# New costs in the account that sets the order of emission of a two-block transformer kernel

## The chip, the cores and the metric

The kernel runs on one NeuronCore of a Trainium2 chip. The metric is the device time of one execution in microseconds (us); several executions are timed and their median is given. TensorE appears in the rows as PE (matmuls) and PEld (weight loads), VectorE as DVE, ScalarE as ACT, GpSimd as POOL, SyncE as SP.

## The reference, cut to what matters

All arithmetic is float32, the batch is 1, the sequence 256 tokens, the model width 2048. A first block works on 272 positions (16 meta tokens ahead of the 256), then a second block of two layers on the 256.

```
block 1:  z  = rmsnorm(h) @ w_in                     # u 1024, q_a 512, kv_a 256, k_pe 64
          ya = s5_mixer(u)                           # 64 groups x 64 complex states
          yb = mla_mixer(q_a, kv_a, k_pe)            # 8 heads
          h += concat(rmsnorm(ya), rmsnorm(yb)) @ w_out
          h += conv_ffn(rmsnorm(h))                  # width 5504
s5_mixer: h[t] = lam_bar * h[t-1] + B u[t];  y = Re(C h) + d * u
          g = gelu(y);  out = g * sigmoid(g @ w_glu + b_glu)
block 2, twice: four mixers of four heads each on one projection (compressed, selected and
          windowed attention; stick breaking; forgetting; differential), w_out,
          then a gated feed-forward net of width 5632 with a convolution of 3 taps
```

The S5 mixer is a linear recurrence along the sequence. Its result passes a GELU before the product with `w_glu` can begin.

## The kernel before, in words

Activations lie transposed in SBUF: features on the 128 partitions, positions along the free axis. Each weight matrix streams in from HBM in halves of 128x1024 floats. A float32 product is made of three passes of the type float32r: the operand is split into a high part (ScalarE copies it to `wh`) and a remainder (VectorE, seldom GpSimd, subtracts: `wl`), and `mm3` issues high by high, low by high and high by low, the lines 633, 634 and 635 of the profile. One 128x512 piece of a weight, one `wh` and one `wl`, feeds 12 passes. `split` makes the pieces and `next` hands them out, up to six pieces ahead (`lead`) in eight buffers.

The instructions of each engine run in the order in which the program emits them (the schedule is manual), so the order of emission is the schedule. Python generators produce it. A main stream emits the big products; beside it stand "sides", generators that emit the S5 steps, the attention heads, the evacuations of PSUM and the norms. The main stream calls `pump` between its products, and `pump` advances every side that is ready.

What is ready is told by an account. Each engine has a clock: `t` for TensorE, `V.clk` for VectorE, `G.clk` for GpSimd, `H.clk` for ScalarE. Every instruction emitted moves the clock of its engine on by a cost worked out from its shape (`_Engine.cost` for the three vector-like engines; `mm`, `mm3`, `mm2` and `mm1` for TensorE), after the clocks at which its operands are written by the account (`_Model.run`). These clocks decide only three kinds of things. A side yields a delay, often `after(V)`: the time until `V.clk` plus 150 ns is reached by `t`. A side is held while `V.clk` or `H.clk` is more than 2700 ns ahead of `t` (`_ok`); the S5 steps have a stricter test, 2500 ns, called `calm`, and the GpSimd part of a step (`post`) is held while `G.clk` is over 1000 ns ahead. And `split` gives a `wl` to GpSimd if `G.clk` is at most 300 ns ahead of `t` and `V.clk` at least 800 ns (in block 1 alone). When the main stream needs a result of a side, `run_until` lets `t` run in steps of 100 ns until it has been emitted.

Block 1 up to the GLU is where most kinds of work run side by side. The main stream emits the projections: u (four pairs of output tiles), q_a, kv_a, k_pe, then the second projections of q, k and v. The S5 side makes 16 steps beside it, two for each tile of 128 channels. A step s is: `bu` (eight TensorE instructions into PSUM banks 4 and 5, operands `s5e` and `s5B`); on VectorE a multiply out of PSUM (`s5ab`), an add (`s5wr`), once more both, and four scans (`s5s`, 128x136); then on GpSimd, in `post`, a multiply `s5pb<-s5s,T` of 128x544 and an add of 128x272 written to a slot named `yl`, each twice. `bu` of step s+1 overwrites the PSUM that the second `s5ab` of step s reads; it is emitted `w_ = self.after(V, extra=0)` after that instruction. Beside the steps, `tables` makes the sines (`tba` and `T`, ScalarE and one VectorE operation per step) and `weights` makes the coefficients of each tile (`s5sm`, `s5C`, GpSimd). After every second step `out` multiplies by C on TensorE. The main stream then comes to the GLU: `gpre` waits until the GELUs of the eight tiles are emitted, so until the last S5 step has been. From there on come the GLU, the product with `w_out` with the attention beside it, and the feed-forward net.

In block 2 the four mixers are sides beside the projections. The stick-breaking mixer (`mix_b`) has a scan of 128x384 for each head, eight in all. GpSimd has little to do there.

Of the kernel before, what the change touches and what calls it, by code (L numbers as in the profile page):

```python
# [25 lines left out]
PSUM = bass.MemoryType.PSUM  # L26
# [262 lines left out]
class _Model:  # L289
# [18 lines left out]
    def run(self, clk, eng, outs, ins, cost, done=60.0):  # L308

        for ap in ins:  # L310
            for k in self.keys(ap):
                w = self.wr.get(k)
                if w is not None:
                    clk = max(clk, w[0] + (0.0 if w[1] == eng else 100.0))
        ok = [k for ap in outs for k in self.keys(ap)]
        for k in ok:
            for d in (self.rd, self.wr):
                w = d.get(k)
                if w is not None and w[1] != eng:
                    clk = max(clk, w[0] + 60.0)  # L320
        clk += cost
        for ap in ins:
            for k in self.keys(ap):
                self.rd[k] = (clk, eng)
        for k in ok:
            self.wr[k] = (clk + done, eng)
        return clk
# [16 lines left out]
class _Engine:  # L344
# [7 lines left out]
    def cost(self, name, out, ins, kw, a):  # L352
        n = 1
        for d in out.shape[1:]:
            n *= d
        if self.name == "V":
            fast = name in ("tensor_scalar", "tensor_copy", "memset") and not any(x.space == PSUM for x in ins)
            return 70.0 + n * (0.52 if fast else 1.04) + (60.0 if name == "tensor_tensor_reduce" else 0.0)
        if self.name == "G":
            if any(isinstance(x, OP) and x == OP.pow for x in a):  # L360
                return 300.0 + 165.0 * n
            return 130.0 + n * (2.15 if len(ins) > 1 else 1.1)
        c = 82.0 if ins and ins[0].space == PSUM else 125.0
        c += 93.0 * sum(not isinstance(kw.get(x, 0.0), (int, float)) for x in ("scale", "bias", "accum_out"))
        f = [x for x in a if isinstance(x, AF) and x in _SETS]
        if f and _SETS[f[0]] != self.set:
            self.set = _SETS[f[0]]
            c += 1283.0
        return c + 0.714 * n

    def __getattr__(self, name):
        f = getattr(self.eng, name)

        def call(out, *a, **kw):
            isap = lambda x: hasattr(x, "ap") and hasattr(x, "space")
            outs = [out] + ([kw["accum_out"]] if "accum_out" in kw else [])
            ins = [x for x in a if isap(x)] + [x for n, x in kw.items() if n != "accum_out" and isap(x)]
            if name == "tensor_tensor_reduce":
                outs.append(ins.pop())
            self.clk = self.k.model.run(self.clk, self.name, outs, ins, self.cost(name, out, ins, kw, a))  # L380
            return f(out, *a, **kw)  # L381

        return call
# [7 lines left out]
class Kern:  # L391
# [109 lines left out]
    def after(self, *engines, extra=150):  # L501

        return max([e.clk for e in engines]) + extra - self.t

    def mm(self, out, lhsT, rhs, start=True, stop=True, n=None, **kw):
        n = n or out.shape[-1]
        if lhsT.dtype != F32:
            c = max(107.0, n / 2.4 + 2.5)
        elif "tile_position" in kw:
            c = 40.0 + 0.4 * n  # L510
        else:
            c = 400.0 if n < 8 else max(220.0, 1.655 * n)
        self.t = self.model.run(self.t, "P", [out], [lhsT, rhs], c)
        self.nc.tensor.matmul(out, lhsT, rhs, start=start, stop=stop, skip_group_check=True, **kw)  # L514
# [114 lines left out]
    def mm3(self, acc, wh, wl, xh, xl, start, stop):  # L629
        nc = self.nc  # L630
        n = acc.shape[-1]
        self.t = self.model.run(self.t, "P", [acc], [wh, wl, xh, xl], 3 * max(109.0, n / 2.4 + 2.5))
        nc.tensor.matmul(acc, wh, xh, start=start, stop=False, skip_group_check=True)  # L633
        nc.tensor.matmul(acc, wl, xh, start=False, stop=False, skip_group_check=True)  # L634
        nc.tensor.matmul(acc, wh, xl, start=False, stop=stop, skip_group_check=True)  # L635

    def mm2(self, acc, wh, wl, xh, start):
        self.t = self.model.run(self.t, "P", [acc], [wh, wl, xh], 2 * max(109.0, acc.shape[-1] / 2.4 + 2.5))
        self.nc.tensor.matmul(acc, wh, xh, start=start, stop=False, skip_group_check=True)
        self.nc.tensor.matmul(acc, wl, xh, start=False, stop=False, skip_group_check=True)  # L640

    def mm1(self, acc, wh, xl):
        self.t = self.model.run(self.t, "P", [acc], [wh, xl], max(109.0, acc.shape[-1] / 2.4 + 2.5))
        self.nc.tensor.matmul(acc, wh, xl, start=False, stop=False, skip_group_check=True)

    def acc4(self, b, n):
# [1787 lines left out]
```

## Time and profile before

| | us |
|---|---|
| median of 3 executions | 3526.95 (3524.05 to 3529.26) |
| profiled execution, its own time | 3522.4 |
| span of the profile, first to last instruction | 3520.6 |
| mean granted TensorE clock, share of full speed | 0.983 |

The profile is one execution. Its own time is 1.8 us above its span. All figures of single instructions come from it, and sums over stages are sums within its span. An instruction that the helper of line 381 emits (all of VectorE, ScalarE and GpSimd) shows that one line, so groups are told apart by the names of their tiles.

### The profile page before, as it was taken

How to read it: one execution, taken by the hardware profiler on the slowest of the kernel's cores; microseconds unless marked ns; L12 is line 12 of the kernel's file. 1: busy time of each engine (PE TensorE's matmuls, PEld its weight loads, DVE VectorE, ACT ScalarE, POOL GpSimd, SP SyncE). 2: the span in 40 equal slices, each digit the busy share in tenths (PEclk: the TensorE clock that was granted, in tenths of full speed). 3: DMA queues.
4: the chain of work that ended last, by engine and by line, in shares of the span. 5: the costliest groups of instructions: out<-in, count | busy, mean ns of one | idle time of the engine just before them, and what ended most of it. 6: DMA issues, size and time to landing. Idle time of an engine off the chain costs nothing.

```text
span 3520.6 us, 70757 instructions
## 1 busy us (share of the span) xinstructions
PE 3391.7 (96%) x27971; PEld 3271.2 (93%) x27971; DVE 2427.7 (69%) x4598; ACT 1714.2 (49%) x3445; POOL 501.0 (14%) x547
## 2 busy tenths in 40 slices
PE   7879999999999999999999999989999999999997
PEld 6768999999999888898999999988899899999997
DVE  7996766666655756558887785565665788888655
ACT  5445544344455555465444444454455544444554
POOL 5652300000000200012000000030000300000002
PEclk9889999999999999999999999999999999999999
DMA  5323455555655564564665556646455455555663
GB/s 176 113 73 104 157 192 177 183 187 176 200 193 184 175 203 151 160 200 147 206 199 194 194 192 194 194 136 230 148 176 171 147 194 195 195 198 195 198 195 126
DMA packets 175022, 618.55 MB, mean 176 GB/s; under 512 B 20224, under 2 KB 24464, under 8 KB 174432
## 3 DMA queue, kind: packets, MB, share of 16 engines
q1 hardware_dynamic: 173488, 612.55, 53.3%
q8 instruction: 219, 3.59, 0.4%
q0 software_dynamic: 336, 0.77, 0.1%
q14 instruction: 115, 0.94, 0.1%
q10 hardware_dynamic: 864, 0.70, 0.1%
HBM read 610.72 MB, written 2.10 MB: 174 GB/s over the span
## 4 chain that ended last, share of the span: by engine, by line
PE 85%; DVE 3%; issue 1%; POOL 1%; ACT 1%; DMA 1%; SPq 0%; ACTq 0%; POOLq 0%; DVEq 0%
PE ps L633 27%; PE ps L634 27%; PE ps L635 27%; PE ps L514 4%; DVE wl L381 1%; POOL acc L381 1%; PE ps L519 1%; DVE X L381 1%; DVE xl L381 0%; DMA wr<-in_w_dram 0%; DVE hb L381 0%; ACT wh L381 0%; DVE xh L381 0%; POOL X L381 0%; ACT hb L381 0%
## 5 line engine op out<-in xcount | busy, mean ns | idle before, releaser
L381 DVE TENSOR_TENSOR wl<-wr,wh 128x512 fp32r<-128x512 f32 (+1 forms) x2000 | 1373.9, 715 | 752.1 <-ACT wh L381 749.1
L381 ACT ACTIVATE wh<-wr 128x512 fp32r<-128x512 f32 (+1 forms) x2014 | 1194.7, 623 | 811.4 <-PE ps L635 378.6
L633 PE MATMUL ps<-xh,wh 128*128 128x256 f32 (+2 forms) x4876 | 1380.2, 283 | 18.1 <-ACT xh L381 8.1
L635 PE MATMUL ps<-xl,wh 128*128 128x256 f32 (+2 forms) x4980 | 1394.0, 280 | 2.9 <-DVE xl L381 2.9
L634 PE MATMUL ps<-xh,wl 128*128 128x256 f32 (+2 forms) x4876 | 1368.2, 281 | 10.8 <-DVE wl L381 10.6
L633 PEld LDWEIGHTS ps<-xh,wh 128*128 128x128 f32 x4876 | 926.9, 190 | 33.1 <-issue 9.7
L635 PEld LDWEIGHTS ps<-xl,wh 128*128 128x128 f32 x4980 | 945.2, 190 | 4.0 <-DVE xl L381 3.8
L634 PEld LDWEIGHTS ps<-xh,wl 128*128 128x128 f32 x4876 | 926.1, 190 | 16.7 <-DVE wl L381 14.8
L633 PE MATMUL ps<-hhh,wh 128*128 128x256 f32 x1820 | 502.1, 276 | 2.3 <-ACT y L381 1.5
L635 PE MATMUL ps<-hhl,wh 128*128 128x256 f32 x1820 | 501.8, 276 | 0.2 <-DVE hhl L381 0.2
L634 PE MATMUL ps<-hhh,wl 128*128 128x256 f32 x1820 | 501.6, 276 | 0.0
L633 PEld LDWEIGHTS ps<-hhh,wh 128*128 128x128 f32 x1820 | 341.7, 188 | 2.7 <-ACT y L381 1.7
L635 PEld LDWEIGHTS ps<-hhl,wh 128*128 128x128 f32 x1820 | 341.6, 188 | 0.4 <-DVE hhl L381 0.4
L634 PEld LDWEIGHTS ps<-hhh,wl 128*128 128x128 f32 x1820 | 341.7, 188 | 0.0
L381 POOL TENSOR_TENSOR acc<-acc,sq 128x256 f32<-128x256 f32 (+1 forms) x137 | 119.2, 870 | 1120.4 <-ACT sq L381 1115.3
L633 PE MATMUL ps<-yh,wh 128*128 128x258 f32 (+2 forms) x696 | 202.3, 291 | 12.4 <-DVE xl L381 8.4
L381 POOL TENSOR_TENSOR hh<-cv,cv 128x256 f32<-128x256 f32 x88 | 84.9, 965 | 852.1 <-DVE cv L381 820.0
L635 PE MATMUL ps<-yl,wh 128*128 128x258 f32 (+2 forms) x696 | 197.9, 284 | 1.7 <-DVE yl L381 1.7
L634 PE MATMUL ps<-yh,wl 128*128 128x258 f32 (+2 forms) x696 | 197.5, 284 | 0.0
L381 DVE SCALAR_TENSOR_TENSOR cv<-pad,cw,cv 128x256 f32<-128x256 f32 x352 | 180.8, 514 | 13.1
L635 PE MATMUL ps<-xl,wxh 128*128 128x256 f32 x588 | 163.9, 279 | 2.3 <-DVE xl L381 2.3
L381 DVE TENSOR_TENSOR wxl<-wr,wxh 128x512 fp32r<-128x512 f32 x230 | 162.6, 710 | 1.9 <-ACT wxh L381 1.9
(449 smaller groups left out, 4351.0 us busy)
## 6 DMA issues: line engine op xcount, KB each, us to landing
wr<-in_w_dram SPq DMA_DIRECT2D x1105, 512.0 KB, 4.7
wr<-in_cmpw_dram SPq DMA_DIRECT2D x32, 512.0 KB, 5.2
wr<-in_w_dram SPq DMA_DIRECT2D x16, 272.0 KB, 4.3
c2t<-in_c_dram SPq DMA_DIRECT2D x2, 1472.0 KB, 9.8
bc<-in_bc_dram SPq DMA_DIRECT2D x8, 256.0 KB, 3.6
X<-in_hT_dram SPq DMA_DIRECT2D x3, 544.0 KB, 9.8
out_dram<-X SPq DMA_DIRECT2D x5, 256.0 KB, 2.2
s5e<-yh SPq DMA_DIRECT2D x64, 17.0 KB, 2.2
```

The costliest lines, as they stand in the source:

```text
L381: return f(out, *a, **kw)
L514: self.nc.tensor.matmul(out, lhsT, rhs, start=start, stop=stop, skip_group_check=True, **kw)
L519: self.nc.tensor.transpose(out, in_, self.ident[:k, :k])
L633: nc.tensor.matmul(acc, wh, xh, start=start, stop=False, skip_group_check=True)
L634: nc.tensor.matmul(acc, wl, xh, start=False, stop=False, skip_group_check=True)
L635: nc.tensor.matmul(acc, wh, xl, start=False, stop=stop, skip_group_check=True)
```

## The change

Only the costs in the account change; no instruction is added, removed or given another shape. A scan is charged 130 + 2.08 n ns in place of 70 + 1.04 n. A VectorE operation with two or more SBUF tensor inputs and a cost over 150 ns is charged up to twice its cost while GpSimd's clock is ahead of VectorE's (`port`). A float32r pass of n columns is charged 113.5 ns per 256 columns, or 0.4427 n + 6, in place of n/2.4 + 2.5 (at least 107 or 109).

```diff
@@ _Engine.cost
         if self.name == "V":
+            if name == "tensor_tensor_scan":
+                return 130.0 + 2.08 * n
             fast = name in ("tensor_scalar", "tensor_copy", "memset") and not any(x.space == PSUM for x in ins)
             return 70.0 + n * (0.52 if fast else 1.04) + (60.0 if name == "tensor_tensor_reduce" else 0.0)
@@ _Engine
+    def port(self, ins, c):
+
+        g = self.k.G.clk - self.clk
+        if self.name == "V" and g > 0 and c > 150 and sum(x.space != PSUM and x.shape[-1] > 1 for x in ins) > 1:
+            return c + min(c, g)
+        return c
+
@@ _Engine.__getattr__, call
-            self.clk = self.k.model.run(self.clk, self.name, outs, ins, self.cost(name, out, ins, kw, a))
+            self.clk = self.k.model.run(self.clk, self.name, outs, ins, self.port(ins, self.cost(name, out, ins, kw, a)))
@@ Kern
+    def one(self, n):
+
+        return 113.5 * max(1.0, n / 256.0) if n % 256 == 0 else 0.4427 * n + 6.0
+
@@ mm
-            c = max(107.0, n / 2.4 + 2.5)
+            c = self.one(n)
@@ mm3 (mm2 and mm1 alike, with 2 and 1 passes)
-        self.t = self.model.run(self.t, "P", [acc], [wh, wl, xh, xl], 3 * max(109.0, n / 2.4 + 2.5))
+        self.t = self.model.run(self.t, "P", [acc], [wh, wl, xh, xl], 3 * self.one(n))
```

## Rows read from the trace of the kernel before

**Rows 1.** The page: busy time of the engines, then tenths busy in 40 slices.

```profile
PE 3391.7 (96%) x27971; PEld 3271.2 (93%) x27971; DVE 2427.7 (69%) x4598; ACT 1714.2 (49%) x3445; POOL 501.0 (14%) x547
...
PE   7879999999999999999999999989999999999997
...
DVE  7996766666655756558887785565665788888655
```

**Rows 2.** Windows: length, busy us (count) by engine, granted PE clock, DMA.

```profile
60.00:262.00 202.00, 158.07 (x1271) 140.60 (x1270) 184.84 (x309) 88.94 (x214) 135.01 (x135) 0.85 0.32 105
262.00:370.00 108.00, 106.78 (x719) 89.75 (x719) 70.67 (x218) 56.74 (x138) 30.09 (x32) 0.99 0.33 106
1200.00:1520.00 320.00, 313.50 (x2250) 277.18 (x2249) 193.02 (x459) 155.18 (x347) 12.53 (x11) 0.99 0.55 177
1640.00:2320.00 680.00, 678.33 (x5982) 677.93 (x5981) 494.32 (x893) 325.02 (x605) 48.62 (x50) 1.00 0.61 196
```

**Rows 3.** Waits from 60 to 262 us: total us, times, longest us.

```profile
ACT T L381 <- DVE tba L381: 51.8, 10, 9.1
POOL s5pb L381 <- DVE s5s L381: 26.6, 10, 5.1
...
PE ps L514 <- DVE s5ab L381: 24.5, 7, 5.7
...
DVE wl L381 <- ACT wh L381: 6.7, 4, 2.5
...
DVE yl L381 <- ACT yh L381: 3.4, 2, 2.2
```

**Rows 4.** DVE groups from 60 to 258 us: busy us, mean ns of one.

```profile
L381 DVE TENSOR_TENSOR wl<-wr,wh 128x512 fp32r<-128x512 f32 x58 | 57.7, 1006 | 6.8 <-ACT wh L381 6.7
L381 DVE TENSOR_TENSOR s5wr<-s5ab 128x272 f32<-128x272 f32 x32 | 33.4, 1042 | 1.1
L381 DVE TENSOR_TENSOR_SCAN s5s<-s5prm,s5wr 128x136 f32<-128x136 f32 x64 | 30.4, 534 | 0.1
L381 DVE TENSOR_TENSOR s5ab<-ps,T 128x544 f32<-128x544 f32 x32 | 23.0, 718 | 0.7
```

**Rows 5.** Tile s5s: ns min/median/max, first and last start.

```profile
L381 DVE TENSOR_TENSOR_SCAN s5s<-s5prm,s5wr x64: 407/416/1005, 69.4 to 254.7; 128x136 f32<-128x136 f32 x64
L381 POOL TENSOR_TENSOR s5pb<-s5s,T x32: 1329/1368/1691, 71.9 to 257.6; 128x544 f32<-128x544 f32 x32
```

**Rows 6.** Tile s5wr, 60 to 258 us, the adds.

```profile
L381 DVE TENSOR_TENSOR s5wr<-s5ab x32: 441/850/1577, 66.2 to 251.0; 128x272 f32<-128x272 f32 x32
```

**Rows 7.** Tile wl, 60 to 258 us, the VectorE subtractions.

```profile
L381 DVE TENSOR_TENSOR wl<-wr,wh x58: 659/795/1905, 59.4 to 257.7; 128x512 fp32r<-128x512 f32 x58
```

**Rows 8.** POOL groups from 60 to 258 us: busy us, mean ns of one.

```profile
L381 POOL TENSOR_TENSOR s5pb<-s5s,T 128x544 f32<-128x544 f32 x32 | 46.7, 1458 | 32.7 <-DVE s5s L381 26.6 <-PE ps L635 3.5 <-DVE tba L381 1.1
L381 POOL TENSOR_TENSOR yl<-s5pb 128x272 f32<-128x272 f32 x31 | 27.3, 882 | 2.4
...
L381 POOL TENSOR_TENSOR wl<-wr,wh 128x512 fp32r<-128x512 f32 x4 | 6.0, 1510 | 11.0 <-ACT wh L381 11.0
```

**Rows 9.** PE timeline, end of the S5 steps: start, us, instruction, idle before.

```profile
244.64 0.61 PE L514 MATMUL ps<-s5e,s5B 64*128 64x136 f32 x3 [0.86 <-DVE s5ab L381]
...
251.30 0.39 PE L635 MATMUL ps<-wl,yh 128*16 128x512 f32 x1
...
260.20 1.58 PE L514 MATMUL ps<-yl,s5C 128*32 128x135 f32 x22 [0.31 <-POOL yl L381]
261.71 0.58 PE L633 MATMUL ps<-yh,wh 128*128 128x258 f32 x1
```

**Rows 10.** DVE groups from 1200 to 1520 us, the scans of mix_b.

```profile
L381 DVE TENSOR_TENSOR_SCAN hb<-hb,c2t 128x384 f32<-128x384 f32 x4 | 3.8, 952 | 3.5 <-ACT hb L381 3.5
```

**Rows 11.** PE timeline, passes of 258 columns on end.

```profile
95.10 0.28 PE L635 MATMUL ps<-xl,wh 128*128 128x258 f32 x1
...
95.47 0.28 PE L635 MATMUL ps<-xl,wh 128*128 128x258 f32 x1
```

More of the change, by code (lines that the diff above doesn't have):

```diff
@@ L637, in mm2 @@
     def mm2(self, acc, wh, wl, xh, start):
-        self.t = self.model.run(self.t, "P", [acc], [wh, wl, xh], 2 * max(109.0, acc.shape[-1] / 2.4 + 2.5))
+        self.t = self.model.run(self.t, "P", [acc], [wh, wl, xh], 2 * self.one(acc.shape[-1]))
         self.nc.tensor.matmul(acc, wh, xh, start=start, stop=False, skip_group_check=True)
@@ L642, in mm1 @@
     def mm1(self, acc, wh, xl):
-        self.t = self.model.run(self.t, "P", [acc], [wh, xl], max(109.0, acc.shape[-1] / 2.4 + 2.5))
+        self.t = self.model.run(self.t, "P", [acc], [wh, xl], self.one(acc.shape[-1]))
         self.nc.tensor.matmul(acc, wh, xl, start=False, stop=False, skip_group_check=True)
```

## Prediction

> **What bounds the kernel now.** I read the page first: TensorE is busy 96% of the span, and its slices are full (8 or 9) everywhere but at the start and at a few short dips [rows 1]. The windows then say which stages have anything to give [rows 2]. From 1640 to 2320 us, a feed-forward stage, TensorE is busy 678.33 of 680 us; a new order can't shorten that. From 1200 to 1520 us, the mixers of the first layer (the second layer repeats it), TensorE idles 320 - 313.5 = 6.5 us. From 262 to 370 us it idles 1.2 us. The exception is 60 to 262 us, the S5 steps beside the projections: TensorE idles 202 - 158.07 = 43.9 us there, its granted clock is 0.85 on average, while VectorE is busy 184.84 of 202 us (92%) and GpSimd 135.01.
>
> So I asked for the waits of that stretch [rows 3]. TensorE's largest is 24.5 us in 7 waits at line 514, for `s5ab` on VectorE: `bu` of the next S5 step is emitted too early and the queue of TensorE stands. That looks like the prize, but its releaser is VectorE, which has hardly any idle time: 202 - 184.84 = 17.2 us, of which 6.7 and 3.4 us are waits for a copy of ScalarE (`wl` for `wh`, `yl` for `yh`). The stretch is bound by VectorE, and TensorE's idle time is what that leaves over. The timeline shows how the stretch ends [rows 9]: the last `bu` at 244.64 us, the last projection pass at 251.30, the last `out` at 260.20 behind GpSimd's add, and from 261.71 on the GLU. Main stream and S5 side end within 10 us of each other, and everything later follows the S5 side's end. What counts is when VectorE has done both lots of work.
>
> Much of VectorE's time is waiting inside instructions. A `wl` takes at least 659 ns and 1006 on average; an `s5wr` add 441 and 1042; a scan 407 and 534 [rows 4 to 7]. All three read two SBUF tensors, while `s5ab`, which reads one of its two from PSUM, shows nothing of the kind (718 ns). The excess over the minimum is 58 x 0.347 + 32 x 0.601 + 64 x 0.127 = 20.1 + 19.2 + 8.1 = 47 us of the 184.84.
>
> **The change part by part.** No instruction is added or removed, so every part acts through the order alone, and costs nothing where the order is not what ends the stage.
>
> *Scans.* The old charge for 136 columns is 70 + 1.04 x 136 = 211 ns, the new 130 + 2.08 x 136 = 413; the shortest in the trace is 407 and the median 416 [rows 5]. For 384 columns 469 becomes 929, and the trace has 952 [rows 10]. A step's four scans move `V.clk` on by 0.81 us more, 12.9 us over 16 steps.
>
> *Port.* Old charges: `wl` 602 ns, `s5wr` 353, scan 413 (new). With GpSimd's clock ahead each is up to doubled, which is about what the trace has (1006, 1042, 534). The account charges only when `G.clk` leads; as VectorE's clock grows faster now, GpSimd leads less often. Doubled for all of them it would be 58 x 0.602 + 32 x 0.353 + 64 x 0.413 = 73 us more, at the least 0; I take 15 us, a fifth, an estimate nearer the low end.
>
> *Passes.* The feed-forward stage has 680 us / 5982 = 113.7 ns for a pass, nearly all of 256 columns [rows 2]; the account goes from 109.2 to 113.5. For 258 columns it goes from 110 to 120.2; three passes on end take 0.37 us, 123 each [rows 11]. So `t` runs 4 to 9% faster against the other clocks, over some 100 us of block 1's projections about 9 us.
>
> What follows from 60 to 262 us, term by term:
>
> (a) `bu` is emitted later, after more passes, and the 24.5 us of waits shrink. Alone this is worth 0 at the end: VectorE is full while TensorE stands. Were VectorE not the bound, it would be up to 24.5; I take 0.
>
> (b) `tables` emits its sines behind `after(V)`. With a short `V.clk` they come too early into ScalarE's queue, which stands 51.8 us in 10 waits for `tba`; the copies `wh` queued behind reach VectorE late, the 6.7 and 3.4 us above [rows 3]. With a longer `V.clk` the sines come later. Between 0 and -10 us; I take -5.
>
> (c) A longer `V.clk` holds the S5 steps back by `calm` while the main stream is not held, so the main stream ends earlier against the S5 side, and the last few steps run with GpSimd as their bound. Per step GpSimd has 135.01 / 16 = 8.4 us; VectorE's own is (57.7 of `wl` left out) (33.4 + 30.4 + 23.0) / 16 = 5.4, with the small operations some 6.7 (estimate). Each step left over idles VectorE by about 8.4 - 6.7 = 1.7 us. Of extra work for VectorE in the account, 12.9 + 15 us, less the 9 us by which `t` is longer, 19 us remain; against 202 us over 16 steps, 12.6 each, that is one or two steps left over. Between 0 and 16 steps x 1.7 = 27 us; I take 2 steps, +3.
>
> (d) `split` gives a `wl` to GpSimd when VectorE's clock leads by 800 ns and GpSimd's by less than 300. VectorE leads more often, so I expect some three more than the 4 now [rows 8]. Each takes 1.0 us off VectorE and puts 1.5 on GpSimd, a third to two thirds of which comes back as waiting on the port. Between 0 and -6 us; I take -1.5.
>
> (e) Elsewhere: `t` 4% faster emits the attention's TensorE work a little early, which can add to the 6.5 us of idle in each layer; 0 to +3 for each, I take +0.5 for both together. The feed-forward stages are full and give 0; the cover there is TensorE's own queue.
>
> The sum is 0 - 5 + 3 - 1.5 + 0.5 = -3 us. Against the profiled execution's own 3522.4 us (span 3520.6 and 1.8 around it) that gives 3519.4. The median of the runs shown, 3526.95, lies 4.55 above that execution, so I predict 3524.
>
> **The rivals.**
>
> *Faster by more.* The accurate order keeps ScalarE and VectorE from standing at all (17.2 us of idle) and lets fewer two-input operations meet GpSimd. All of the idle and a tenth of the 47 us would be 22 us; two thirds of that, about -14, gives 3513. For it: the releasers of the idle are instructions emitted early. Against it: GpSimd has 135 us of work in 202 whatever the order, so most meetings stay.
>
> *Slower.* `calm` closes too long, and the S5 side falls far behind. In the tail a step alone is then a chain: 0.61 us of `bu` [rows 9], 2 x 0.72 + 2 x 0.44 of VectorE, 4 x 0.41 of scans, and on GpSimd (46.7 + 27.3) / 16 = 4.6, in all 9.2 us where VectorE has 6.7 to do, so 2.5 us lost a step. With 9 steps left over that is 22.5 us; less the 6.5 of (b) and (d), +16: 3543. It decides from about 6 steps left over, where 6 x 2.5 passes the 6.5 us gained and the 7 us of the bound below. Against it: evacuations and norms stop the main stream too by the same held sides, so the two can't part far.
>
> *GpSimd is held too.* The new account lets VectorE wait for GpSimd and not the reverse. The trace has `s5pb` at 1329 ns at least and 1458 on average [rows 5, 8], so GpSimd loses 32 x 0.13 = 4 us to something over the stretch, uncharged. If the held-back S5 steps gather at the end, where GpSimd is the bound, these 4 us come on top of (c): 3528. The Trainium skill has the rule ("SBUF — State Buffer", section "Who interferes with whom"): a VectorE instruction with two SBUF inputs and a GpSimd instruction that reads SBUF exclude each other, and the one that comes second waits until the first has ended. By that rule the trace agrees on both sides, 1006 ns against 659 for `wl` and 1458 against 1329 for `s5pb`, and an account with one side of it is half right.
>
> *Nothing moves.* The queues are ordered as before where it matters, and the time is 3527. The gates of the account work on differences of clocks, and all of them grow together.
>
> **How the numbers follow.** Forecast (-10 to +6 around -3) 0.40; faster by more 0.25; slower 0.20; GpSimd held too 0.08; nothing moves 0.07. A difference of 0.2%, 7 us, is about what a measurement can tell here. Of the forecast's own range some 0.11 lies beyond -7 and nothing beyond +6; the rest of it, GpSimd held too and nothing moves are within, 0.44, less 0.03 that GpSimd's 4 us may carry over the bound. Faster 0.36, same 0.41, slower 0.23. The range reaches halfway into both rivals and beyond: 3509 to 3541.
>
> **What the next profile would show.** Right: the 24.5 us of TensorE's waits for `s5ab` mostly gone; ScalarE's 51.8 us for `tba` lower; VectorE still about 90% busy between 60 us and the GLU, and the GLU's steady start within 7 us of 261.71; the last projection pass further ahead of the last `out` than 9 us; from there to the end the same length. Wrong: a start of the GLU 15 us away on either side, VectorE under 85% busy before it (the tail), or idle time of TensorE in the layers' mixers well over 6.5 us each.

## The result, and the profile after

The changed kernel takes 3549.01 us (median of 8 runs, 3541.05 to 3571.92); the kernel before, run beside it on the same chip, 3527.2 (8 runs, 3524.05 to 3529.97). The ratio is 1.0065, 95% interval 1.0046 to 1.0084: slower by 0.65%. The prediction was 3524 us, with a range of 3509 to 3541.

The profiled execution of the changed kernel is one of its longer ones: its own time is 3563.27 us, its span 3561.5. To see where it falls behind I used that each trace holds the same 26,148 passes of the main stream, so that the same pass can be looked up in any timeline. "The loss at pass N" below (counted from 1) is the start of pass N less its start in the kernel before. Two other kernels that keep the order of before in block 1 stand between -1.0 and +1.7 us up to pass 2401, so a loss of one or two microseconds can't be told from nothing.

| main stream's pass | where | before, us | loss after, us |
|---|---|---|---|
| 948 | last projection | 251.3 | 3.0 |
| 997 | GLU, running steadily in every trace | 268.1 | 11.0 |
| 1189 | `w_out`, behind its wait for the GLU's last results | 293.4 | 15.8 |
| 2401 | feed-forward of block 1 | 482.6 | 17.9 |
| 10,201 | end of the mixers, first layer | 1525.5 | 18.7 |
| 15,001 | up-projections of the first feed-forward net | 2086.8 | 38.9 |
| 26,148 | the last | 3500.7 | 40.9 |

So there are two losses: 17.9 us in block 1 up to the attention, and 20 us between 1525 and 2090 us, most of it at a steady rate. The second comes and goes between executions of one kernel (last section), so part of the 21.8 us between the medians is not the change's. Without it the shortest executions fit: 3541.05 - 3524.05 = 17.0 us. What has to be explained is block 1.

The windows of the changed kernel, same stretches as [rows 2] (length, busy us and count by engine, granted clock, DMA):

```profile
60.00:262.00 202.00, 159.98 (x1266) 143.19 (x1268) 182.79 (x295) 89.07 (x214) 134.04 (x135) 0.86 0.32 104
262.00:370.00 108.00, 97.92 (x653) 80.91 (x646) 69.72 (x197) 49.98 (x125) 33.20 (x31) 0.93 0.28 89
1200.00:1520.00 320.00, 313.99 (x2246) 277.05 (x2245) 197.32 (x469) 157.16 (x353) 13.97 (x14) 0.99 0.54 180
1640.00:2320.00 680.00, 676.98 (x5795) 676.28 (x5794) 491.52 (x888) 316.33 (x581) 48.45 (x54) 1.00 0.59 190
```

From 60 to 262 us nothing looks different by the shares: VectorE is 90% busy here as it was 92% before. But 295 of its instructions were run where 309 had been, in nearly the same busy time. From 262 to 370 us TensorE now idles 10.1 us where it idled 1.2, and its granted clock is 0.93 where it was 0.99: the S5 steps reach into that stretch.

The waits from 60 to 262 us, against [rows 3]:

```profile
ACT T L390 <- DVE tba L390: 45.9, 10, 8.9
...
POOL s5pb L390 <- DVE s5s L390: 15.7, 11, 4.9
DVE wl L390 <- ACT wh L390: 15.5, 9, 4.0
PE ps L527 <- DVE s5ab L390: 13.9, 4, 5.3
...
DVE yl L390 <- ACT yh L390: 1.0, 2, 0.8
```

The waits that the change was to remove did shrink: TensorE's for `s5ab` from 24.5 to 13.9 us, ScalarE's for `tba` from 51.8 to 45.9. VectorE's own wait for `wh` grew instead, from 6.7 to 15.5; that for `yh` went from 3.4 to 1.0.

The end of the S5 steps, against [rows 9] (timeline of TensorE):

```profile
254.27 0.39 PE L648 MATMUL ps<-wl,yh 128*16 128x512 f32 x1
256.37 1.19 PE L527 MATMUL ps<-s5e,s5B 64*128 64x136 f32 x8 [1.71 <-DVE s5ab L390]
...
274.77 1.13 PE L527 MATMUL ps<-yl,s5C 128*32 128x135 f32 x32
```

The last projection pass is 3.0 us later than before and the last `bu` 11.7; the last `out` ends at 275.90 us, 14.1 later.

VectorE is the busiest engine of the stretch, so its time up to the GLU is added up first. In the texts below "the GLU's start" is counted back from pass 997 by 48 passes of 0.12 us: 262.3 us before, 273.2 after. The windows from 0 to there, before and after:

```profile
0.00:262.30 262.30, 200.93 (x1561) 179.59 (x1562) 227.44 (x410) 125.09 (x295) 164.36 (x170) 0.89 0.37 121
```

```profile
0.00:273.20 273.20, 210.47 (x1551) 188.99 (x1552) 233.43 (x407) 125.16 (x295) 173.68 (x177) 0.86 0.35 116
```

Of the 10.9 us, VectorE's busy time makes 6.0 (227.4 to 233.4) and its idle time 4.9 (34.9 to 39.8). The two add up to the window by definition, so they divide the delay and do not explain it. The groups of VectorE in these windows show which instructions grew (busy us, mean ns; the scans and adds of before are those of [rows 4], its `wl` first here):

```profile
L381 DVE TENSOR_TENSOR wl<-wr,wh 128x512 fp32r<-128x512 f32 x81 | 75.1, 941 | 14.9 <-ACT wh L381 14.7
```

```profile
L390 DVE TENSOR_TENSOR wl<-wr,wh 128x512 fp32r<-128x512 f32 x76 | 69.1, 924 | 21.1 <-ACT wh L390 20.5 <-PE ps L648 0.4
L390 DVE TENSOR_TENSOR_SCAN s5s<-s5prm,s5wr 128x136 f32<-128x136 f32 x64 | 44.2, 748 | 0.0
L390 DVE TENSOR_TENSOR s5wr<-s5ab 128x272 f32<-128x272 f32 x32 | 31.2, 974 | 1.1
```

The same 64 scans take 44.2 us where they took 30.4. The tile's own view says how: the shortest is unchanged (407 ns in [rows 5]), the median nearly doubled from 416.

```profile
L390 DVE TENSOR_TENSOR_SCAN s5s<-s5prm,s5wr x64: 406/782/2048, 73.2 to 266.7; 128x136 f32<-128x136 f32 x64
```

Laid beside GpSimd's instructions, each of the 33 scans above 500 ns overlaps one of GpSimd, and of the 31 shorter ones 29 overlap none. Before there were 18 such long scans, again each with an overlap, and 44 of the other 46 had none. Overlaps with a `wl` on GpSimd went from 0 to 7, those with the S5 steps' own multiplies and adds (`s5pb<-s5s,T` and `yl`) from 3 to 14. The scans, the same 64 as before, gained 13.8 us of waiting, and `s5wr` lost 2.2. Of the 6.0 us that `wl` lost, 4.7 are its five instructions fewer (81 to 76, at 941 ns), and only 1.3 come from a shorter mean. The order that charges for meetings on the port has more of them, and the scans bear the increase.

### The profile page after: what moved, and what is told of

It reads as the page before. It is cut to its first block, busy times and chain, and to the rows that moved or that the text cites. A ratio compares the mean times of both kernels' runs of the same rounds, so it can differ in the third digit from the quotient of the medians.

```text
span 3561.5 us, 70788 instructions
## 1 busy us (share of the span) xinstructions
PE 3428.6 (96%) x27971; PEld 3305.4 (93%) x27971; DVE 2435.2 (68%) x4590; ACT 1714.9 (48%) x3445; POOL 510.8 (14%) x555
## 4 chain that ended last, share of the span: by engine, by line
PE 87%; DVE 7%; ACT 2%; issue 2%; POOL 2%; DMA 1%; SPq 0%; ACTq 0%; DVEq 0%; POOLq 0%
PE ps L646 27%; PE ps L648 27%; PE ps L647 27%; PE ps L527 5%; DVE wl L390 2%; DVE s5s L390 1%; POOL acc L390 1%; PE ps L532 1%; DVE X L390 1%; DVE xl L390 1%; ACT wh L390 1%; DVE s5ab L390 0%; DMA wr<-in_w_dram 0%; DVE s5wr L390 0%; DMA wr<-in_cmpw_dram 0%
## 5 line engine op out<-in xcount | busy, mean ns | idle before, releaser
L390 DVE TENSOR_TENSOR wl<-wr,wh 128x512 fp32r<-128x512 f32 x1992 | 1368.8, 716 | 780.4 <-ACT wh L390 776.6
L390 DVE SCALAR_TENSOR_TENSOR cv<-pad,cw,cv 128x256 f32<-128x256 f32 x352 | 180.8, 514 | 13.1
```

## The experiments

All kernels were timed beside the kernel before on one chip for each group: it took 3528.43 us with the first four, 3529.87 with the next four, then 3528.2, 3530.46 and 3528.96. The place of a loss was read from the passes of one profiled execution. The letters of the theories hold within one group. "The account" is the program that sets the order.

**Where: block 1 or the layers.** The new costs are applied only up to the end of the GLU's passes, or only from there on (A: the loss lies in block 1):

```
+    new = True                      # the other kernel: False
-            if name == "tensor_tensor_scan":
+            if self.k.new and name == "tensor_tensor_scan":
...
         s5st.close()                # end of the GLU's passes
+        self.new = False            # the other kernel: True
```

(`port` and `one` are switched in the same way.)

> New costs up to the end of the GLU, old costs from there on. Computes the same result. Theory A (the loss lies in the S5 stretch: the S5 steps are held back and end later, 277.6 us in the changed kernel's profile against 261.7): about 16 us slower than before, 3541 to 3546, and the steady start of the GLU near 277 us. Theory B (the loss is made in the layers, by attention work emitted early and by a slower rhythm of the passes there, 117.7 ns a pass against 113.3 in layer 0's feed-forward net): within 5 us of before, 3522 to 3532. If the executions spread as widely as the changed kernel's (3541 to 3572), the rhythm does not hang on the order in the layers.

> Old costs up to the end of the GLU, new costs from there on. Computes the same result. Theory A: the GLU's steady start stays at 262 us and the time at 3527, give or take 4. Theory B: 10 to 30 us slower, and as wide a spread as the changed kernel's 31 us.

The first took 3541.85 us (ratio 1.0031, 1.0007 to 1.0056) and has a loss of 10.6 us at pass 997 and 15.9 at pass 2401, nearly that of the changed kernel. The second took 3528.82 (0.9998, 0.9971 to 1.0025) and stays within 1 us of before at both passes. A was right on the time and the place (it had the GLU's start at 277 us, and it came at 272.9). The loss is made in block 1; in the layers the new costs do nothing that these times, good to some 0.25%, can tell.

**Which part.** Scans, port and passes one at a time, the other two with the old costs:

> Only the scans' new charge; port and passes as before. Computes the same result. Theory A1 (the longer scans hold the S5 side back most): last two S5 products on TensorE both after the last projection pass, GLU start at 270 us or later, 3535 to 3545. Theory A2 (the port charge does it): 3525 to 3531.

> Only the port charge; scans and passes as before. Computes the same result. Theory A1: 3525 to 3531. Theory A2: GLU start at 270 us or later, 3535 to 3545. If both this and the scans alone are slower, the two work through the same test of VectorE's clock and either is enough.

> The account of before, with the costs of the TensorE passes alone taken as new; all values are computed as before. By the account the sixteen bu are emitted after 258 to 888 passes of the main stream (before 264 to 930, after 252 to 948), and GpSimd is given 15 wl in block 1 (before 14, after 22). Theory A (what costs is that the account holds the S5 steps, so that the last one is emitted when the main stream has run out): last bu near 240 us as before, GLU start within 3 us of 261.7, time within 5 us of before. Theory B (what costs is the wl that GpSimd is given: each stretches scans on VectorE, which is the engine with the most work there): one wl more, so nothing either, within 5 us. Theory C (the true pass costs alone make the order worse): GLU start at 270 or later, 10 us or more above before.

Loss at passes 997 and 2401: scans 1.8 and 4.2 us (3527.0, ratio 0.9988, 0.9968 to 1.0009), port 3.2 and 6.0 (3529.84, 1.0005, 0.998 to 1.0029), passes 7.0 and 10.2 (3537.07, 1.0017, 0.9996 to 1.0039). Neither the scans nor the port alone makes the loss, so A1 and A2 are both out. The passes alone make half of it by another way: there the S5 steps are early (last `out` done at 259.2 us, before 261.8) and the projections late, pass 948 by 11.8 us. So the lateness of the S5 side, theory A of that group, isn't a necessary part; C was nearer, with 269.2 us where it asked for 270.

**GpSimd's subtractions, and the hold.** In the second group A says that steps held too long cost the time, B that the `wl` given to GpSimd stretch VectorE's scans. One number is changed in each:

```
 # kernel before
-        eng = ... self.V.clk >= self.t + 800 ...
+        eng = ... self.V.clk >= self.t + 300 ...
 # changed kernel
-        calm = lambda: V.clk <= self.t + 2500 and H.clk <= self.t + 2500
+        calm = lambda: V.clk <= self.t + 3500 and H.clk <= self.t + 3500
 # changed kernel
-        eng = ... self.V.clk >= self.t + 800 ...
+        eng = ... self.V.clk >= self.t + 1500 ...
```

> The kernel before with one number changed: split gives a wl to GpSimd when VectorE's clock is 300 ns ahead, where it was 800 ns. By the account the sixteen bu keep their places (264 to 930 passes) and GpSimd gets 20 wl instead of 14. Theory A (held steps): same places, so no loss, within 3 us of before, GLU start at 261 to 263 us. Theory B (GpSimd's wl stretch the scans): six wl leave VectorE (about 0.9 us each, -5 us) and six GpSimd operations of 1.4 us stretch scans and others; the 64 scans up to the GLU take over 42 us (before 34.2, after 47.9), VectorE's busy sum rises, GLU start 5 to 10 us later, 3532 to 3537.

> The changed kernel with one number changed: the S5 steps are held when a clock is 3500 ns ahead of TensorE's, where it was 2500. By the account the first fourteen bu keep the places of after; the last two come after 912 and 930 passes, where they came after 939 and 948; GpSimd gets 20 wl instead of 22. Theory A (held steps): the last step is taken up while the main stream still runs; last bu at 246 to 250 us instead of 256, GLU start 6 to 10 us earlier than in after, time 3538 to 3543. Theory B (wl on GpSimd): two wl fewer, scans still above 45 us up to the GLU, GLU start within 3 us of after, time within 3 us of after.

> The changed kernel with one number changed: split gives a wl to GpSimd when VectorE's clock is 1500 ns ahead, where it was 800. By the account GpSimd gets 13 wl (before 14, after 22); the bu come at 252 to 582 as in after, then at 708, 738, 786, 816, 864, 876, 888, 906 (after 720 to 948). Theory A: the last step comes earlier even than in before, so the last bu at 240 to 246 us and the GLU at 262 to 268 us; the time 3527 to 3534. Theory B: scans near 35 to 38 us up to the GLU and VectorE's busy sum back at 251 us, with the same time; where the scans stay above 44 us and the time falls all the same, B is out, and where the scans fall and the time stays, A is out.

The first gave GpSimd only one `wl` more between 60 and 258 us, so it hardly puts B to the test: scans 30.4 us as before, loss 2.0 us at both passes, 3526.96 us (1.0, 0.9978 to 1.0023). The second moved the last `bu` from 256 to 250 us and the loss at pass 997 from 11.0 to 4.6 us, as A said; but 14.8 us stand at pass 2401, and it takes 3541.23 us (1.0036, 1.0011 to 1.0061). Of these, 7.2 are lost in the attention: TensorE waits 1.5 us for ScalarE there, and then its granted clock is 0.50 for 10.2 us, 100% busy, which costs about half of that (an estimate). The third fails both: with 13 `wl` on GpSimd by the account the scans fall to 39.5 us only, VectorE's busy time to 229.7, and its idle time rises to 43.4; loss 10.9 and 22.3 us, 3548.11 us (1.0056, 1.0037 to 1.0074). Its attention too has 10.2 us at a clock of 0.50, from 343.3 us on. The loss does not hang on the extra `wl` of GpSimd.

**The GLU's own part; the limits; the port.** The next four: new costs only until the last S5 step is emitted; the changed kernel with both limits 1000 ns looser; and both kernels without GpSimd's multiplications.

```
 # new costs up to the last S5 step (gpre)
                 self.run_until(lambda: s5.done)
+                self.new = False
 # limits
-        lag = self.t + 2700                  # calm: 2500
+        lag = self.t + 3700                  # calm: 3500
 # no multiplication: G.only charges the account and issues nothing
-                G.tensor_tensor(Pb, sr, T if c == 0 else T[:, 1::-1], OP.mult)
-                G.tensor_tensor(hs[c], Pb[:, 0], Pb[:, 1], (OP.add, OP.subtract)[c])
+                G.only(Pb, sr, T if c == 0 else T[:, 1::-1])
+                G.only(hs[c], Pb[:, 0], Pb[:, 1])
+                G.eng.tensor_tensor(hs[c], sr[:, 0], sr[:, 1], (OP.add, OP.subtract)[c])
```

"Time over the usual" in these expectations is, for each VectorE instruction, its duration less that of the shortest twentieth of its kind, summed up to the GLU's start.

> New costs only until the last S5 step has been emitted, old ones from the GLU on; all values as before. In after the loss against before grows to 11.0 us by the GLU's start, by another 4.8 us at the GLU's end (the pass after it) and 2 us in the attention. Theory G (the account's new costs inside the GLU make its end late): start of the GLU still +11 us, its end adds nothing, +11 to +12 us from 430 us on, time about 3537. Theory S (the S5 side leaves VectorE with work left over, and that makes the GLU's end late whatever the account says there): +4 to +5 us at the end of the GLU here too, +16 us from 430 us on, time about 3542.

> The changed kernel with the limits at which sides are held loosened by 1000 ns each: any side 3700 ns ahead (was 2700), S5 steps 3500 ns (was 2500). By the account step 4's bu then comes after 414 passes (after: 462, before: 420), step 8's at 648 (720, 582), the last at 912 (948, 930); GpSimd gets 12 wl (22, 14). Theory H (steps held by charged port waits leave VectorE idle): VectorE's idle time from 50 to 150 us falls from 14.2 us back to 8 to 9, GLU start at 262 to 267 us (before 262.3, after 273.2), 6 to 11 us of the loss gone there. Theory P (the order puts scans and subtractions beside GpSimd's operations, so VectorE's instructions take longer): VectorE's time over the usual time of each instruction stays at 75 to 80 us up to the GLU (before 69.9, after 79.2), GLU start above 269 us.

> The kernel before with GpSimd's 32 multiplications by the sines (128x544) left out of the S5 steps: the following add reads the scans directly, so the S5 outputs are other values. The account still charges them, so the order of all else is that of before. Theory P: VectorE's 69.9 us over the usual times up to the GLU fall by about a third, as GpSimd's 42.6 of 167 us leave it, by 15 to 25 us, and since VectorE is busy 87% of the time the GLU starts 10 to 20 us earlier. If VectorE's lengthened instructions cost nothing: the GLU starts within 3 us of 262.3.

> The changed kernel with the same 32 multiplications left out and still charged (S5 outputs are other values), order as in after. Theory P: its 79.2 us fall further than before's 69.9, and the distance of the GLU starts (10.9 us between after and before) shrinks to 2 to 6 us between this kernel and the one before it. Theory H (held steps alone): the distance stays at 9 to 13 us.

*The GLU.* Loss 10.7 us at pass 997 as in the changed kernel, but 12.5 at pass 1189 and 13.1 at pass 2401, where that has 15.8 and 17.9: 3541.76 us (1.0033, 1.0012 to 1.0054). By the trace G holds for the larger share: of the 6.9 us lost behind pass 997, 4.5 come from the new costs in the GLU and the attention, 2.4 come with the S5 order. The median is the one that S gave (3542). TensorE's waits at the GLU's end, from 286 to 310 us, in the changed kernel and in this one:

```profile
PE ps L646 <- ACT yh L390: 3.9, 2, 2.6
```

```profile
PE ps L649 <- ACT yh L390: 1.7, 2, 0.9
PE ps L651 <- DVE yl L390: 0.4, 1, 0.4
```

The waits are not all of it. As the last of them ends TensorE's granted clock falls to 0.50 (1.2 GHz), for 6.8 us in the changed kernel and 3.4 in this one; in the kernel before it is 1.00 (2.4 GHz) from 264.3 to 400 us. Windows of the three, in that order:

```profile
305.50:312.30 6.80, 6.58 (x30) 6.45 (x31) 5.70 (x33) 2.04 (x5) 2.29 (x2) 0.50 0.45 154
```

```profile
303.70:307.10 3.40, 3.03 (x14) 2.94 (x14) 2.54 (x5) 2.55 (x5) 0.12 (x1) 0.50 0.31 93
```

```profile
264.30:400.00 135.70, 134.48 (x956) 117.26 (x956) 93.98 (x257) 74.23 (x174) 38.12 (x41) 1.00 0.38 123
```

At 0.50 the passes of 258 columns start 0.215 us apart, at 1.00 0.12, so the 6.8 us cost about 3.0 (an estimate). With 2.7 us more of waits at the GLU's end than before and 1.5 in the attention this makes about the 6.9.

*The limits.* The loss falls to 1.4 us at pass 997 and 3.6 at pass 2401; 3528.28 us (1.0011, 0.9987 to 1.0034). H called the sum right, but not the way: from 50 to 150 us the idle time fell from 14.6 to 11.3 us only, where it said 8 to 9. VectorE's window up to the GLU:

```profile
0.00:263.70 263.70, 207.31 (x1547) 186.40 (x1551) 223.31 (x407) 122.57 (x289) 167.47 (x171) 0.85 0.36 119
```

Its idle time stays at 40.4 us (39.8 in the changed kernel); what fell is the busy time, from 233.4 to 223.3. The scans went from 44.2 to 35.1 us, the `s5wr` from 31.2 to 27.4; the time over the usual from 79 to 66 us. P, which said that it would stay, is out in that form.

*The port.* Without the 32 multiplications the window up to the GLU, first with the order of before, then with the new one:

```profile
0.00:234.50 234.50, 195.45 (x1559) 175.88 (x1559) 194.70 (x408) 122.74 (x290) 115.47 (x138) 0.91 0.40 134
```

```profile
0.00:250.40 250.40, 201.97 (x1551) 181.97 (x1552) 203.27 (x407) 125.42 (x295) 125.88 (x145) 0.89 0.38 127
```

Taking 49 us from GpSimd took 32.7 us from VectorE, which lost no instruction, and brought the GLU 27.8 us forward, both more than P said (15 to 25 and 10 to 20). So much of VectorE's time hangs on this work of GpSimd in the kernel before (`wl` 941 to 775 ns, `s5wr` 1042 to 609). GpSimd's own part of each step became shorter too, and what share of the 27.8 us is due to that is not told apart. The whole time fell to 3502.5 us with the old order (0.9914, 0.989 to 0.9939; two executions only) and 3515.31 with the new (0.9965, 0.9949 to 0.9982). But the distance between the two orders did not shrink, as P asked: it grew from 10.9 to 15.9 us, with 8.6 of busy time and 7.3 of idle. The scans alone make 8.5 of the 8.6 (38.1 us with the new order, 29.6 with the old). So the multiplications left out are not what separates the two orders, and the other work of GpSimd lengthens the scans as well.

**Is it the limits, or the draw?** In the fourth group, L says that the limits are too tight for the new costs, O that each setting only draws another order. Both limits by -1000 and +1000 ns with the old costs, +500 and +2000 with the new:

```
-        lag = self.t + 2700                  # calm: 2500
+        lag = self.t + 3700                  # old costs; calm 3500
+        lag = self.t + 1700                  # old costs; calm 1500
+        lag = self.t + 3200                  # new costs; calm 3000
+        lag = self.t + 4700                  # new costs; calm 4500
```

> The kernel before with both limits loosened by 1000 ns (sides 3700 instead of 2700, S5 steps 3500 instead of 2500), all values as before. By the account the bu of steps 14 and 15 then come after 948 passes, when the main stream has run out (before 921 and 930), step 8's after 732 (582). Theory L (2700 and 2500 are too tight only for the higher new costs): with old costs nothing is gained or lost, GLU start within 3 us of before's 262.3, time within 4 us. Theory O (each setting is another draw of the order, some good, some bad, with either account): GLU start anywhere from 260 to 274 us, and by its late last steps more likely late, 266 to 272 us.

> The kernel before with both limits tightened by 1000 ns (1700, 1500). By the account step 4's bu comes after 480 passes (before 420, after 462), step 8's after 696 (582, 720), the last after 921 (930, 948). Theory L: a tighter limit with old costs acts as higher costs with the old limit, and brings the loss: GLU start 268 to 274 us, 3534 to 3545. Theory O: anywhere from 260 to 274 us, by its early last step more likely 262 to 267.

> The changed kernel with both limits loosened by 500 ns (3200, 3000). By the account the last bu comes after 894 passes (after 948), step 8's after 618 (720), step 4's after 444 (462). Theory L: part of the loss undone, GLU start between the 273.2 us of after and the 263.7 us at 3700, so 265 to 270 us. Theory O: 260 to 274 us; by the main stream, which has 54 passes left behind the last step, the projections end late instead, as in the run with the passes alone, 267 to 271 us.

> The changed kernel with both limits loosened by 2000 ns (4700, 4500). By the account step 4's bu comes after 438 passes, step 8's after 744, the last after 930 (after 462, 720, 948; before 420, 582, 930). Theory L: at least as good as at 3700, GLU start 260 to 265 us, 3522 to 3530. Theory O: 260 to 274 us, and by its middle steps, which stand as late as after's, more likely 266 to 272 us.

| order of block 1 | loss at pass 997 | at pass 2401 | VectorE busy, idle to the GLU's start | median, ratio |
|---|---|---|---|---|
| before | 0 | 0 | 227.4, 34.9 | |
| changed | 11.0 | 17.9 | 233.4, 39.8 | 3549.01, 1.0065 |
| new costs, limits +500 | 11.0 | 14.6 | 222.3, 51.0 | 3540.03, 1.0028 (1.0002 to 1.0054) |
| new costs, limits +1000 | 1.4 | 3.6 | 223.3, 40.4 | 3528.28, 1.0011 |
| new costs, limits +2000 | 1.8 | 4.4 | 223.6, 40.5 | 3526.51, 0.9995 (0.9966 to 1.0023) |
| old costs, limits +1000 | 4.0 | 8.9 | 230.9, 35.4 | 3537.64, 1.003 (1.0001 to 1.006) |
| old costs, limits -1000 | 0.9 | 1.0 | 227.2, 36.1 | 3546.45, 1.0044 (1.0021 to 1.0067) |

L fails three times. With +500 the start of the GLU gains nothing, though VectorE's busy time falls by 11 us, since its idle time grows by as much; 12.2 us of idle lie after 220 us, where it waits mostly for ScalarE's `yh` and `wh`. The looser limit with the old costs does lose, 4.0 us and then 8.9. The tighter one with the old costs does not bring the loss in block 1; what that kernel loses, it loses later: 9 us of its trace at the steady rate of the last section, 8 in the second layer's mixers. L holds for +2000 alone. O is left, a scatter without relation to the limit, but its range of 260 to 274 us is so wide that it could hardly fail (the starts were 266.3, 263.2, 273.3 and 264.1). O's own guesses from the places of the `bu` held for the two with the old costs and failed for the two with the new.

**A version of both.** At +2000 the loss fell by 3.7 us in the second layer's mixers, from 4.1 at 2380 us to 0.4 at 2600, so the last kernel keeps the old costs and limits up to the end of the GLU's passes and takes the new costs with 4700 ns from there:

```
-        lag = self.t + 2700
+        lag = self.t + (4700 if self.new else 2700)
```

> Old costs and old limits until the GLU's passes are emitted, from there on the new costs with sides held at 4700 ns (S5 steps stand in the old part); all values as before. By the account the first 1654 instructions come as in before and the last 15964 of 18109 as in the run with the new costs and the limit at 4700. If the 3.6 us are made by the order in block 2: within 1 us of before until 2300 us, 3 to 4 us ahead of it from 2700 us on, median 3520 to 3526, ratio 0.998 to 1.000. If they were a chance of that one execution, or given back by another place: within 1.5 us of before at the end, ratio 0.9995 to 1.001.

It took 3524.66 us against 3528.96 (0.9986, 0.9963 to 1.0009). In its trace the gain in the second layer's mixers is there again, at 2.6 us (loss 28.1 at 2380 us, 25.5 at 2690; 24 of the 28 are the steady rate, between 1680 and 2380 us, and 1.7 the attention). By 2850 us 2.0 of the 2.6 are lost again (27.5). So the gain stands in two traces at that place, is mostly given back in the second, and the times can't tell it from nothing.

## Why the prediction was wrong

*The bound* was read rightly for these two orders: VectorE stays 90% busy up to the GLU, and TensorE's waits are leftover. Term (a) held as well: 10.6 of the 24.5 us of those waits went, and nothing came of it. It does not hold for every order: with the limits at +500 VectorE is busy 5 us less than before, and the GLU starts 11 us later.

*The step that failed* is the sum's treatment of VectorE's busy time. No term lets the waiting inside its instructions change, apart from the share that (d) takes back; the prediction gives its reason under the rival "faster by more", that GpSimd has its work whatever the order, so most meetings stay. The port paragraph sizes only what the account charges. The sum has -1.5 us there, by (d). VectorE's busy time rose by 6.0 instead, with scans +13.8 us, `wl` -6.0 and `s5wr` -2.2. GpSimd was given six more `wl` between 60 and 262 us, 10 for 4, where (d) counted three more; what that took from VectorE was less than the scans gained. That the meetings can shift by this much is shown from both sides: up to the GLU's start VectorE is busy between 222 and 234 us in the orders run. The prediction had 47 us of such waiting in plain sight and treated it as fixed. The rest of the GLU's 10.9 us is idle time of VectorE, +4.9 where (b) and (c) together had -2.

*(b)* had the wrong sign. ScalarE's wait for `tba` fell by 5.9 us as said, but VectorE's waits for `wh` and `yh` went from 10.1 to 16.5 us, +6.4 where -5 was taken. While S5 steps are held, VectorE has `wl` and small operations in its queue and stands for some of the `wh`. In the timeline, the scans of the step whose `s5wr` were done at 100 us come at 114:

```profile
98.89 1.57 DVE L390 TENSOR_TENSOR s5wr<-s5ab 128x272 f32<-128x272 f32 x1
...
108.04 0.69 DVE L390 TENSOR_TENSOR wl<-wr,wh 128x512 fp32r<-128x512 f32 x1 [1.64 <-ACT wh L390]
...
111.74 0.69 DVE L390 TENSOR_TENSOR wl<-wr,wh 128x512 fp32r<-128x512 f32 x1 [2.06 <-ACT wh L390]
...
113.98 2.40 DVE L390 TENSOR_TENSOR_SCAN s5s<-s5prm,s5wr 128x136 f32<-128x136 f32 x3
```

*(c)* counted the steps left over about right (two forecast; one `bu` comes after the last projection pass, another 3 us ahead of it) and priced them too low: between pass 948 and the GLU 7.9 us were lost where 3 were taken. *(e)* was +0.5 for the layers, which nothing here contradicts, but it passed over the GLU's end and block 1's attention, which lost 6.9 us, some 3 of them (an estimate, above) by the granted clock.

*Of the signs* that it gave for being right, VectorE's 90%, ScalarE's shorter waits and the greater distance between the last projection pass and the last `out` (20.5 us for 9) came. TensorE's waits for `s5ab` fell by 43% and not mostly, the GLU started more than 7 us later, and from there on the length grew. Two rows were misread on the way. The 0.61 us of `bu` are three of its eight passes (1.19 us in all), and the doubled charges, 1204, 706 and 826 ns, do not fit what the trace has (1006, 1042, 534).

*The rival "slower"* gave 3543, close to the shortest executions (3541), but by luck, as the mechanism is another: not nine steps left over but one or two, and busy time as much as idle. The rival "GpSimd is held too" shows nothing: `s5pb` took 1423 ns from 60 to 262 us, where it had taken 1458. The rule cited there (the Trainium skill, "SBUF — State Buffer", section "Who interferes with whom") agrees with the overlaps of the long scans and with the runs without the multiplications: VectorE with unchanged work was busy 32.7 us less when GpSimd was busy 49 us less. As a guide to order this account of it did not serve: with it the scans have 13.8 us more of waiting.

*What stays open* is which property of an order makes it good. Of the 14 other orders of block 1 that were run (three share the S5 part), none stands ahead of that of before at pass 2401; they lose 1.0 to 22.3 us (the middle ones 8.9 and 10.2), and only the smallest two, 1.0 and 2.0, can't be told from nothing. The scans alone lose 4.2 us, the port 6.0, the passes 10.2, and all three at once 17.9; looser limits undo most of it at +1000 and +2000 and little at +500. An order can be late in two ways. In three (passes alone, new costs with 1500 ns, limits +500) the last projection pass comes 12 to 16 us late, and the GLU starts 6.1 us behind it; in all others the GLU starts within 3 us of the end of the last `out`. Neither the places of `bu`, nor the number of `wl` on GpSimd, nor the length of the scans sorts the orders: old costs with limits at -1000 have 41.7 us of scans and lose 1.0, new costs with +500 have 36.2 and lose 14.6.

## What to carry to other kernels

A truer account is first of all another order and need not be a better one: here none of 14 other orders was better in the stage concerned, and 12 lost 3.6 us or more. Whether the order before was itself picked among several is not known here; where one was, expect a new one to lose. In a stage bound by an engine that shares a port, put its busy time, not only its idle time, among the things that an order can change: it moved by 12 us here with the same instructions. To place a loss, follow the same instruction by its number through both traces; this placed to a microsecond or two what shares and waits left unclear. And look at the granted clock behind a wait of TensorE, which can cost as much again: here three kernels ran 6.8 to 10.2 us at 0.50 behind waits of 1.5 to 3.9 us.

## What was unexpected of the hardware

TensorE, 100% busy at a granted clock of 1.00, runs the same passes of 256 columns at one of two rates. The windows from 1640 to 2080 us, before and after:

```profile
1640.00:2080.00 440.00, 440.00 (x3885) 440.00 (x3884) 357.75 (x658) 204.88 (x372) 42.09 (x42) 1.00 0.61 197
```

```profile
1640.00:2080.00 440.00, 437.12 (x3698) 436.64 (x3697) 343.48 (x628) 200.30 (x363) 42.41 (x48) 1.00 0.59 189
```

That is 113.3 ns an instruction before and 437.12 / 3698 = 118.2 after, nearly all of them passes of 256 columns. From the start of one such pass to the next it is 113.3 and 117.8 ns, which makes 16 us between 1680 and 2090 us. The run with the new costs and the limits at +1000 has the longer step in its trace in the same stretch, four others for 210 to 240 us between 2070 and 2330 us (new costs from the GLU on, old costs with limits at -1000, and the two without the multiplications), and the last kernel in both stretches, 24 us in all; the other traces don't. The order alone doesn't decide it: of the ten times of the kernel with +1000, seven lie between 3523.72 and 3529.41 us and three between 3545.64 and 3554.79, and the one that was traced with the longer step is of the three (3545.64). The kernel before has such executions as well, up to 3555.17 us beside the first four. What sets the rate was not tried.
